# Two half quanta per slot, a later output tail in linear attention, query and key projections spread among the gates, and keys fetched in pieces, in a two-layer hybrid attention kernel

## The chip, the cores and the metric

The kernel runs on one core of one Trainium2 chip. The metric is device time in microseconds from start to end of one execution; the time before is the median of three runs.

## The reference

Two layers over 1024 latent tokens and 256 context tokens of width 1024; the output is the latents after the second layer. Per layer (`ctx` is the same with its own modulation, and has an output in the first layer only):

```python
h = rms_norm(x, norm_w) * (1.0 + scale) + shift
(na_q, na_k, na_v, gla_q, gla_k, gla_v, gla_g, ret_q, ret_k, ret_v, z, g) = split_cols(h @ w_in)
...
q = rms_norm(split_heads(q, NA_HEADS), q_norm); k = rms_norm(split_heads(k, NA_HEADS), k_norm)
na_l = neighbourhood_attention(ql, kl, vl, kc, vc, rpb)   # 8x16 windows on a 16x64 grid, plus all context keys
gla_l = bidir_scan(...)   # gated linear attention, a decay per key channel, forward and backward
ret_l = bidir_scan(...)   # retention, a fixed decay per head
y = sum(sigmoid(gs[i]) * ((outs[i] * silu(zs[i])) @ w_branch[i]) for i in range(3))
x = x + gate * (y @ w_out)
```

Columns of `w_in`: 3 × 512 for neighbourhood attention (8 heads of 64), 256 + 256 + 512 + 32 for linear attention, 1024 for retention, 1536 for z and 3072 for the gates g.

## The kernel before, in words

Every projection runs as a stream of matmuls in fp32 with weights split into a high and a low part (`whi`, `wlo`), three products per tile: activations' high part by both, their low part by `whi` (`fm_unit`, `tm_unit`, the matmul at L374 in `mms`). Weights come in groups of 256 columns; `conv` (L333) splits them on ACT (L340) and POOL (L343). A group of queries and keys, of gates or of z is two halves of 128 columns; in layer 0 each half runs over 512 + 512 + 256 tokens, in layer 1 the gates, z and the queries run over 512 + 512 only. One such block is a tile with its own bank of PSUM: three banks (`pg`) hold projection results, five (`pa`) hold those of the background.

The order of all instructions is written by hand, by a driver (`Drv`, L49 to L103). One generator yields the projections (`stream`), lanes yield the three branches, which spawn units ("workers"): retention chunks, linear attention chunks, neighbourhood attention units. A slot (`Drv.slot`, L81) steps each worker once, issues projection matmuls up to the quantum, runs late work and evacuations of finished tiles, steps the lanes, steps each worker again, runs the tail work, and last the weight loader. `mms` yields when `QUANT * drv.mult` columns are issued (L366): 6144 columns are twelve 512-wide matmuls. `drv.mult` is set by the branch that runs: 1.25 in retention, 1.1, 1.2 and 1.0 in linear attention (`GL_M`), 0.65 in neighbourhood attention (`NA_M1`). Linear attention falls from 1.2 to 1.0 once `d["done"]["nqk"]` is set (L857).

`projections` (L1089) takes, in this order: retention's, linear attention's and the values' columns, the four groups of queries and keys (`nqk`), twelve groups of gates, six of z. The fifth and sixth z group wait until the neighbourhood lane is at its end (`want_E`). A tile of queries or keys goes through `qk_evac` (L1151): COPY and Square on ACT (L1154, L1155), the mean over a head by a matmul with `blk` (L1160, `na_ms`), Ln, Exp and Square on ACT (L1162 to L1164), products on DVE (L1167 to L1182), the low part on POOL (L1186), and the stores of `nq`, `nkh`, `nkl` to DRAM. A gate tile is one Tanh (L1211, `st_g`).

Linear attention's `phase2` (L757) takes chunks of 128 tokens, one spawned every 8 slots. For seven levels it makes a decay (`dd`, exponential at L796), scaled queries and keys on DVE (`ek`, `eq`, L805 to L807) and a product on PE (`gla_lv`, L824), which ACT or DVE merges into `att`. Then come `gla_o` (L848) and `post` (L467): a copy into a staging buffer `posb`, mean squares on ACT and POOL, a scaling on DVE (L482), a transposition (`post_t`, L486), a gain and a store.

Neighbourhood attention (L863) goes over four pairs of heads; a pair has eight window units and, in layer 0, two context units. A unit (`pair`, L974) loads `q`, `qz` and the bias `bt`, then on PE: scores in four banks (`na_sw`, `na_sc`, L901, L902); softmax on DVE and ACT (L917 to L922 and L933 to L935); transposes (`na_ptw`, `na_ptc`, L944, L947); copies out on DVE and ACT (L966, L969, `PT`); and the product with the values (`na_o`, L1012). Each pair's `k0`, `k1` and `kl` (128 × 1280 floats each, 640 KB) are fetched during the pair before, one whole tile per unit from the fourth unit on, in the queue of SP.

## Time and profile before

| | |
|---|---|
| median of three runs | 3006.08 us (3004.04 to 3006.4) |
| the profiled execution | 3011.38 us |
| its span, first to last instruction | 3009.5 us |
| mean granted clock of TensorE | 0.976 |
| PE busy | 2850.7 us, 95% of the span |
| DVE, ACT, POOL busy | 1517.4, 1061.7, 1082.0 us |

Durations come from the profiled execution, which is 5.3 us above the median. PE's busy time counts matmuls; they overlap in the pipe, so a row's length is more than what it adds to the time: the distance between two rows' starts tells that. A wait is named by the instruction that waits and the one that released it.

### The profile page before, as it was taken

Reading aid. Unit: us, or ns where it says so; the run is one execution under the profiler, and the core shown is the slowest. Engines: PE = TensorE matmul, PEld = TensorE weight load, DVE = VectorE, ACT = ScalarE, POOL = GpSimd, SP = SyncE. Lnnn points to the kernel's source line nnn. Section 1 sums busy time; section 2 is a strip of 40 time slices with the busy share of each in tenths; the row PEclk is TensorE's granted clock in tenths of the full one; section 3 lists DMA queues with packets and bytes.
Section 4 is the critical chain, followed back from the end, with each engine's and each line's share of the span. In section 5 each row is a group of like instructions: output and inputs, shape, how many; then the busy total and the mean of one; then the engine's idle time right before and its main releaser. Section 6 shows DMA issues by size and latency. Waiting matters only on the chain. (4 is left out here: it accounts for less than half of the span.)

```text
span 3009.5 us, 52036 instructions
## 1 busy us (share of the span) xinstructions
PE 2850.7 (95%) x19776; PEld 2441.5 (81%) x19776; DVE 1517.4 (50%) x3261; ACT 1061.7 (35%) x2443; POOL 1082.0 (36%) x1010
## 2 busy tenths in 40 slices
PE   7999999899988899999999999999899978899999
PEld 5999987678877778778899999986677767777889
DVE  4147478866534555224333337378966255632431
ACT  5123465543333444212113223365544334432220
POOL 4222125565410102433655332115665210135463
PEclk8999999999999999999999999999899989999999
DMA  6244443433244454666445354443433445555633
GB/s 236 85 151 127 134 126 102 121 97 123 86 150 146 147 158 126 195 188 206 140 127 148 97 151 125 122 135 109 123 99 116 146 145 154 164 163 159 209 120 107
DMA packets 381161, 418.69 MB, mean 139 GB/s; under 512 B 33308, under 2 KB 298284, under 8 KB 380912
## 3 DMA queue, kind: packets, MB, share of 16 engines
q1 hardware_dynamic: 343552, 361.59, 39.9%
q10 hardware_dynamic: 37360, 53.79, 5.1%
q8 instruction: 156, 2.56, 0.4%
q14 instruction: 93, 0.76, 0.1%
HBM read 302.72 MB, written 112.54 MB: 138 GB/s over the span
## 5 line engine op out<-in xcount | busy, mean ns | idle before, releaser
L374 PE MATMUL fm<-h,whi 128*128 128x512 f32 (+1 forms) x3936 | 917.4, 379 | 0.0
L343 POOL TENSOR_TENSOR wlo<-wraw,whi 128x512 fp32r<-128x512 f32 (+1 forms) x336 | 461.5, 1394 | 1144.5 <-ACT whi L340 1086.5
L374 PEld LDWEIGHTS fm<-h,whi 128*128 128x128 f32 x3936 | 679.2, 191 | 142.8 <-issue 18.6
L374 PE MATMUL fm<-h,wlo 128*128 128x512 f32 (+1 forms) x1968 | 473.9, 378 | 0.0
L374 PEld LDWEIGHTS fm<-h,wlo 128*128 128x128 f32 x1968 | 342.5, 191 | 74.4 <-issue 12.2
L374 PE MATMUL tm<-whi,h 128*128 128x256 f32 (+1 forms) x2528 | 345.5, 285 | 2.4 <-ACT h L293 1.7
L374 PEld LDWEIGHTS tm<-whi,h 128*128 128x128 f32 x2528 | 321.4, 190 | 4.1 <-ACT h L293 2.1
L340 ACT CAST whi<-wraw 128x1024 fp32r<-128x1024 f32 (+1 forms) x168 | 175.4, 1047 | 289.4 <-PE tm L374 128.9
L374 PE MATMUL tm<-wlo,h 128*128 128x256 f32 (+1 forms) x1264 | 181.3, 285 | 0.0
L374 PEld LDWEIGHTS tm<-wlo,h 128*128 128x128 f32 x1264 | 164.2, 190 | 0.0
L1211 ACT ACTIVATE st_g<-fm 128x512 f32<-128x512 f32 (+1 forms) x120 | 66.5, 554 | 231.9 <-PE fm L374 177.0
L374 PE MATMUL tm<-whi,yy 128*128 128x256 f32 x1152 | 147.4, 280 | 0.0
L1227 DVE SCALAR_TENSOR_TENSOR st_z<-st_z,fm 128x512 f32<-128x512 f32 (+1 forms) x60 | 38.0, 634 | 214.5 <-ACT st_z L1226 211.7
L805 DVE TENSOR_TENSOR ek<-dd,kd 128x512 f32<-128x512 f32 x108 | 106.7, 988 | 68.8 <-ACT dd L796 68.5
L374 PEld LDWEIGHTS tm<-whi,yy 128*128 128x128 f32 x1152 | 140.8, 188 | 0.1
L781 POOL TENSOR_TENSOR dd<-Ac,ash 128x256 f32<-128x256 f32 x126 | 108.3, 860 | 88.3 <-DVE ash L768 56.8
L414 DVE COPY st_tm<-tm 128x256 f32<-128x256 f32 (+1 forms) x59 | 25.3, 429 | 174.0 <-PE tm L374 173.7
L824 PEld LDWEIGHTS gla_lv<-eq,ek 128*64 128x64 f32 x2016 | 70.8, 140 | 51.8 <-issue 29.9
L782 POOL TENSOR_TENSOR dd<-ash,Ac 128x256 f32<-128x256 f32 x126 | 110.9, 880 | 0.0
L1348 DVE TENSOR_TENSOR st_o<-tm,gb 128x256 f32<-128x256 f32 x72 | 30.5, 424 | 155.0 <-PE tm L374 120.7
L806 DVE SCALAR_TENSOR_TENSOR eq<-dd,g_col,qd 128x256 f32<-128x256 f32 x126 | 104.9, 832 | 6.5 <-ACT dd L796 6.5
L1294 DVE SCALAR_TENSOR_TENSOR gt<-gt,mg 128x512 f32<-128x512 f32 (+1 forms) x80 | 50.7, 634 | 110.9 <-PE mg L374 89.1
(1570 smaller groups left out, 4705.2 us busy)
## 6 DMA issues: line engine op xcount, KB each, us to landing
wraw<-in_w_in SPq DMA_DIRECT2D x104, 512.0 KB
wt<-in_w_mod SPq DMA_DIRECT2D x48, 512.0 KB
gd<-st_g ACTq DMA_DIRECT2D x96, 256.0 KB
gt<-gd SPq DMA_DIRECT2D x96, 256.0 KB
bt<-in_na_bm SPq DMA_DIRECT2D x32, 384.0 KB
ot<-o SPq DMA_DIRECT2D x48, 256.0 KB
wraw<-in_w_branch SPq DMA_DIRECT2D x24, 512.0 KB
k<-nkh SPq DMA_DIRECT2D x16, 640.0 KB
```

Source lines behind the costliest of these rows:

```text
L340: sc.copy(hi[:, :, :w], raw[:, :, :w])
L343: gp.tensor_tensor(lo[:, ks, :w], raw[:, ks, :w], fv(hi[:, ks, :w]), op=ALU.subtract)
L374: pe.matmul(ps, a(k), b(k), start=i == 0, stop=i == tot - 1)
L781: gp.tensor_tensor(dv[:, :, Lh:], av[:, :, Lh:], rv, op=ALU.subtract)
L782: gp.tensor_tensor(dv[:, :, :Lh], rv, av[:, :, :Lh], op=ALU.subtract)
L805: ve.tensor_tensor(ek_, E_, kd_, op=ALU.mult)
L806: ve.scalar_tensor_tensor(eq[:, :, Lh:], ev[:, :, Lh:], rsc, qv[:, :, Lh:], op0=ALU.mult, op1=ALU.mult)
L824: pe.matmul(pl_[bk, h, :], ek_[:, h, bk], eq_[:, h, bk if lv else bq], start=True, stop=True)
L1211: sc.activation(st[:, :nn], ps, AF.Tanh, scale=0.5)
L1227: ve.scalar_tensor_tensor(st[:, :nn], st[:, :nn], 1.0, ps, op0=ALU.add, op1=ALU.mult)
L1294: ve.scalar_tensor_tensor(gt[:, :nn], gt[:, :nn], 1.0, ps[:, :nn], op0=ALU.add, op1=ALU.mult)
L1348: ve.tensor_tensor(st[:, :256], ps, gbc[0 if t < LT else 1][:, 256 * gi:256 * gi + 256], op=ALU.mult)
```

## The change

A slot steps the workers, issues a half quantum (3072 columns times `drv.mult`), and does both again; late work, evacuations, lanes, tail and loader follow, and the second stepping of the workers behind the lanes is gone. `post` takes its buffer and two lags: retention keeps (2, 1), linear attention has (5, 2) and works in `att`. The exponential `qi` is written into `Ac`. `load_k` fetches five pieces of 256 tokens of each of its three tiles (128 KB each), three pieces per unit from the third unit on. In `projections` a group of queries and keys goes ahead of each of the first four pairs of gate groups, and `done["nqk"]` is set after the seventh gate group. In `qk_evac` the buffer `rs` is taken later and the mean-square product one step later. The list of groups, which sets the order of weight loading, follows.

```diff
--- before.py
+++ after.py
@@ -80,10 +80,11 @@
 
     def slot(self, gemm=True):
         self.n += 1
-        self._adv(self.workers)
         alive = False
-        if gemm:
-            alive = next(self.gemm, "end") != "end"
+        for _ in range(2):
+            self._adv(self.workers)
+            if gemm:
+                alive = next(self.gemm, "end") != "end"
         for f in self.late:
             f()
         self.late, self.later = self.later, []
@@ -91,7 +92,6 @@
             f()
         self.evq, self.evq_next = self.evq_next, []
         self._adv(self.lanes)
-        self._adv(self.workers)
         for f in self.tail:
             f()
         self.tail = []
@@ -363,7 +363,7 @@
                 load_raw()
             conv()
 
-    QUANT = 6144
+    QUANT = 3072
     acc = [0]
 
     def mms(ps, n, pairs, kd):
@@ -437,8 +437,12 @@
         G["gla"] = [add_group(wcols(1792, 256), KD), add_group(wcols(2048, 272), KD), add_group(wcols(2320, 272), KD),
                     add_group(wcols(1536, 256), KD)]
         G["nv"] = [add_group(wcols(1024, 256), KD), add_group(wcols(1280, 256), KD)]
-        G["nqk"] = [add_group(wcols(p * P, P) + wcols(512 + p * P, P), KD) for p in range(4)]
-        G["g"] = [add_group(wcols(5152 + 256 * i, 256), KD) for i in range(12)]
+        G["nqk"], G["g"] = [], []
+        for i in range(12):
+            if i % 2 == 0 and i < 8:
+                p = i // 2
+                G["nqk"].append(add_group(wcols(p * P, P) + wcols(512 + p * P, P), KD))
+            G["g"].append(add_group(wcols(5152 + 256 * i, 256), KD))
         G["z"] = {zi: add_group(wcols(3616 + 256 * zi, 256), KD) for zi in (2, 3, 4, 5, 0, 1)}
         G["wb"] = {br: [add_group([(A["w_branch"][layer, br][:, 256 * i:256 * i + 256], 256)], 4) for i in range(4)]
                    for br in BR_ORDER}
@@ -464,9 +468,8 @@
     xnew = [dr.tile([P, D], F32, tag=f"xn{t}", name=f"xn{t}") for t in range(NT)]
 
 
-    def post(pool, ops, gain, o_d, c):
+    def post(pool, ops, gain, o_d, c, osb, lag):
         ss = pool.tile([P, 12], F32, tag="pss", name="pss", bufs=2)
-        osb = stg("posb")
         on = osb.rearrange("p (h d) -> p h d", h=4)
 
         def squares():
@@ -477,15 +480,16 @@
             gp.tensor_scalar(ss[:, 4:8], ss[:, 0:4], 1.0 / P, EPS, op0=ALU.mult, op1=ALU.add)
             gp.tensor_tensor(ss[:, 8:12], ss[:, 4:8], mhalf, op=ALU.pow)
         drv.tail.append(squares)
-        yield
-        yield
+        for _ in range(lag[0]):
+            yield
         ve.tensor_tensor(on, on, ss[:, 8:12].unsqueeze(2).to_broadcast([P, 4, P]), op=ALU.mult)
-        yield
+        for _ in range(lag[1]):
+            yield
         pt = psa("post_t", (P, 4, P))
         for h in range(4):
             pe.transpose(pt[:, h, :], on[:, h, :], ident)
         yield
-        of = stg("pof")
+        of = osb if lag[0] > 2 else stg("pof")
         ve.tensor_tensor(of.rearrange("p (h t) -> p h t", h=4), pt, gain.unsqueeze(2).to_broadcast([P, 4, P]), op=ALU.mult)
         drv.defer(lambda: dma(o_d.rearrange("(h d) t -> d h t", d=P)[:, :, c * P:(c + 1) * P], of.rearrange("p (h t) -> p h t", h=4)))
 
@@ -619,7 +623,7 @@
                     pe.matmul(po[:, hs], att[:, h // 2, h % 2, :], v[:, hs], start=True, stop=False)
                     pe.matmul(po[:, hs], q2T[:, h // 2, h % 2, :], S[:, c, hs], start=False, stop=True)
                 yield
-                yield from post(pr, po, gain, d["o"][2], c)
+                yield from post(pr, po, gain, d["o"][2], c, stg("posb"), (2, 1))
 
             drv.mult = RT_M
             ws = []
@@ -809,7 +813,7 @@
                         vt = pl.tile([P, 512], F32, tag="v", name="vt", bufs=2)
                         dma(vt, d["gla"][c * P:(c + 1) * P, 0:512])
                     if i == 6:
-                        qi = stg("qi").rearrange("p (h t) -> p h t", h=4)
+                        qi = Ac
                         sc.activation(qi, Ac, AF.Exp, scale=s_pm)
                         ve.tensor_tensor(qi, qi, qd, op=ALU.mult)
                     yield
@@ -848,7 +852,7 @@
                     pe.matmul(po[:, hs], att[:, h, :], vt[:, hs], start=True, stop=False)
                     pe.matmul(po[:, hs], qi[:, h, :], S[:, c, hs], start=False, stop=True)
                 yield
-                yield from post(pl, po, gain, d["o"][1], c)
+                yield from post(pl, po, gain, d["o"][1], c, att.rearrange("p h t -> p (h t)"), (5, 2))
 
             ws = []
             for c in range(d["nt"]):
@@ -872,16 +876,17 @@
                 gp.memset(fv(qz[:]), 0.0)
 
             def load_k(p):
-                ks = []
-                for hd in range(2):
-                    k = pn.tile([P, NTOK], F32R, tag=f"k{hd}", name=f"k{hd}", bufs=2)
-                    r = p * P + 64 * hd
-                    dma(fv(k[:]), d["nkh"][r:r + 64, :].unsqueeze(0).to_broadcast([2, 64, NTOK]))
-                    ks.append(k)
-                    yield
+                ks = [pn.tile([P, NTOK], F32R, tag=f"k{hd}", name=f"k{hd}", bufs=2) for hd in range(2)]
                 kl = pn.tile([P, NTOK], F32R, tag="kl", name="kl", bufs=2)
-                dma(fv(kl[:]), d["nkl"][p * P:(p + 1) * P, :])
                 tiles["k", p] = ks, kl
+                for t0 in range(0, NTOK, 256):
+                    ts = slice(t0, t0 + 256)
+                    for hd in range(2):
+                        r = p * P + 64 * hd
+                        dma(fv(ks[hd][:, ts]), d["nkh"][r:r + 64, ts].unsqueeze(0).to_broadcast([2, 64, 256]))
+                        yield
+                    dma(fv(kl[:, ts]), d["nkl"][p * P:(p + 1) * P, ts])
+                    yield
 
             def load_v(p):
                 vcx = pn.tile([P, 2, P], F32, tag="vcx", name="vcx", bufs=2)
@@ -1048,7 +1053,7 @@
                 for n, unit in enumerate(heads(p)):
                     ws.append(drv.spawn(unit))
                     yield
-                    if n > 2:
+                    for _ in range(3 if n > 1 else 0):
                         next(nxt, None)
                     yield
                 for _ in nxt:
@@ -1150,12 +1155,14 @@
 
         def qk_evac(p):
             def f(m, t0, nn, ps):
-                raw, sq, rs = stg("nraw"), stg("nsq"), stg("nrs")
+                raw, sq = stg("nraw"), stg("nsq")
                 sc.copy(raw[:, :nn], ps)
                 sc.activation(sq[:, :nn], raw[:, :nn], AF.Square)
 
                 def w():
                     yield
+                    yield
+                    rs = stg("nrs")
                     pm_ = psa("na_ms")
                     pe.matmul(pm_[:, :nn], blk, sq[:, :nn], start=True, stop=True)
                     yield
@@ -1199,12 +1206,6 @@
                 drv.spawn(w())
             return f
 
-        for p in range(4):
-            yield from fm(G["nqk"][p], [ntok, NTOK], qk_evac(p))
-        yield
-        yield
-        d["done"]["nqk"] = True
-
         def g_evac(gi):
             def f(m, t0, nn, ps):
                 st = stg("st_g")
@@ -1214,7 +1215,11 @@
             return f
 
         for gi in range(12):
+            if gi % 2 == 0 and gi < 8:
+                yield from fm(G["nqk"][gi // 2], [ntok, NTOK], qk_evac(gi // 2))
             yield from fm(G["g"][gi], [ntok] * 2, g_evac(gi))
+            if gi == 6:
+                d["done"]["nqk"] = True
 
         def z_evac(zi):
             def f(m, t0, nn, ps):
```

What moves, in the order of the program. First ACT, in layer 0, where tiles of queries and keys are evacuated beside linear attention: `nraw` and the first `nsq` are COPY and Square of a tile, `nrs` its Ln and Exp, `dd` linear attention's exponential. Before (lines of the kernel before):

```order
L796 ACTIVATE dd<-dd 128x512
L1162 ACTIVATE nrs<-na_ms,eps_t 128x512
L1163 ACTIVATE nrs<-nrs 128x512
L1164 ACTIVATE nsq<-nrs 128x512
L1154 COPY nraw<-fm 128x256
L1155 ACTIVATE nsq<-nraw 128x256
L796 ACTIVATE dd<-dd 128x512
L1162 ACTIVATE nrs<-na_ms,eps_t 128x512
L1163 ACTIVATE nrs<-nrs 128x512
L1164 ACTIVATE nsq<-nrs 128x512
L340 CAST whi_6378<-wraw_6108 128x4x256
```

With the change, in a group that follows gates (L1169 is the Ln, L1170 the Exp):

```order
L800 ACTIVATE dd<-dd 128x512
L117 DMA gd_99<-st_g 128x256
L832 COPY near<-gla_lv 128x256
L800 ACTIVATE dd<-dd 128x512
L1169 ACT_TABLE_LOAD
L1169 ACTIVATE nrs<-na_ms,eps_t 128x512
L1170 ACT_TABLE_LOAD
L1170 ACTIVATE nrs<-nrs 128x512
L1171 ACTIVATE nsq<-nrs 128x512
L1159 COPY nraw<-fm 128x512
L1160 ACTIVATE nsq<-nraw 128x512
L1159 COPY nraw<-fm 128x256
```

Between a tile's Ln and its Exp, and ahead of the Ln, stand loads of ACT's table that were not there; in the whole program the loads go from 5 to 71.

Second, PE in linear attention's chunks of layer 0: the level products (`gla_lv`) and the projection matmuls between them. Before, after the queries and keys:

```order
L824 MATMUL gla_lv<-eq,ek 64x64 x8
L374 MATMUL fm<-h_0_141,whi_6378 128x512 x4
L374 MATMUL fm<-h_4_142,whi_6534 128x512 x4
L374 MATMUL fm<-h_8_143,whi_6378 128x512 x4
L824 MATMUL gla_lv<-eq,ek 64x64 x8
L374 MATMUL fm<-h_12_144,whi_6534 128x512 x4
L374 MATMUL fm<-h_0_141,wlo_6379 128x512 x4
L374 MATMUL fm<-h_4_142,wlo_6535 128x512 x4
L824 MATMUL gla_lv<-eq,ek 64x64 x8
```

With the change, among the gates and the remaining queries and keys:

```order
L828 MATMUL gla_lv<-eq,ek 64x64 x8
L374 MATMUL fm<-h_0_141,whi_7297 128x512
L374 MATMUL fm<-h_4_142,whi_7510 128x512 x4
L374 MATMUL fm<-h_8_143,whi_7297 128x512 x4
L374 MATMUL fm<-h_12_144,whi_7510 128x512 x4
L374 MATMUL fm<-h_0_141,wlo_7298 128x512 x3
L828 MATMUL gla_lv<-eq,ek 64x64 x8
```

Between two level products stood 12 projection matmuls, and now stand 16 as long as `nqk` isn't done.

Third, PE in neighbourhood attention of layer 0. Before, between all units of the stage:

```order
L901 MATMUL na_sc<-k_9439,q 128x256
L902 MATMUL na_sc<-kl,qz_8960 128x256
L374 MATMUL fm<-h_0_141,wlo_9562 128x512 x4
L374 MATMUL fm<-h_4_142,wlo_9753 128x512 x4
L944 MATMUL na_ptw<-ident,P__10612 128x128 x3
L947 MATMUL na_ptc<-ident,P__10612 128x128 x2
L944 MATMUL na_ptw<-ident,P__10619 128x128 x3
L947 MATMUL na_ptc<-ident,P__10619 128x128 x2
L374 MATMUL fm<-h_0_145,whi_9561 128x512 x4
L374 MATMUL fm<-h_4_146,whi_9752 128x512 x4
L1012 MATMUL na_o<-PT,vw 64x128 x6
L1012 MATMUL na_o<-PT,vcx 64x128 x4
```

With the change, the last projection matmuls of the stage (the fourth z group's) and what follows them:

```order
L374 MATMUL fm<-h_8_150,whi_10452 128x256 x4
L374 MATMUL fm<-h_8_150,whi_10622 128x256 x4
L374 MATMUL fm<-h_0_149,wlo_10453 128x256 x4
L374 MATMUL fm<-h_0_149,wlo_10623 128x256 x4
L1017 MATMUL na_o<-PT,vw 64x128 x6
L1017 MATMUL na_o<-PT,vcx 64x128 x4
L906 MATMUL na_sw<-k_10838,q 128x384
L907 MATMUL na_sw<-kl,qz_9351 128x384
L906 MATMUL na_sw<-k_10839,q 128x384
L907 MATMUL na_sw<-kl,qz_9351 128x384
L906 MATMUL na_sc<-k_10838,q 128x256
L907 MATMUL na_sc<-kl,qz_9351 128x256
```

From there the units' products follow one another without a projection matmul, over 13 window units and 4 context units in layer 0, and over 19 window units in layer 1; before, projection matmuls stood between the units in both layers to the end of the stage.

## Rows read from the trace of the kernel before

**Rows 1.** The page's first part: span, and busy time of each engine.

```profile
span 3009.5 us, 52036 instructions
PE 2850.7 (95%) x19776; PEld 2441.5 (81%) x19776; DVE 1517.4 (50%) x3261; ACT 1061.7 (35%) x2443; POOL 1082.0 (36%) x1010
```

**Rows 2.** PE's waits over the whole span: the waiting instruction, what released it, us in total, number, longest.

```profile
PE na_o L1012 <- ACT PT L969: 47.6, 7, 14.5
...
PE post_t L486 <- DVE posb L482: 14.6, 5, 5.7
PE gla_lv L824 <- DVE eq L807: 13.9, 8, 4.1
...
PE na_ms L1160 <- ACT nsq L1155: 9.3, 5, 3.6
```

**Rows 3.** Stretches of the span: length, busy us of PE, PEld, DVE, ACT and POOL (instructions), granted clock, DMA share, GB/s. Linear attention with queries and keys in layer 0, neighbourhood attention in layer 0, and both in layer 1.

```profile
400.00:650.00 250.00, 226.59 (x1544) 179.41 (x1543) 207.25 (x349) 135.40 (x267) 126.94 (x126) 0.97 0.38 111
850.00:1160.00 310.00, 277.26 (x1965) 236.06 (x1964) 165.08 (x537) 128.45 (x421) 27.44 (x21) 0.94 0.49 150
1950.00:2200.00 250.00, 227.38 (x1540) 182.18 (x1539) 204.77 (x363) 136.35 (x257) 116.05 (x106) 0.97 0.41 116
2350.00:2660.00 310.00, 270.18 (x1791) 224.36 (x1790) 170.56 (x511) 119.81 (x386) 36.89 (x27) 0.92 0.51 155
```

**Rows 4.** The chain of waits in neighbourhood attention of layer 1: start, us, what.

```profile
2391.87 17.55 DMA k<-nkh
...
2478.82 24.30 DMA k<-nkh
```

**Rows 5.** ACT's groups between 400 and 650 us, the instructions of a tile of queries or keys: busy us, mean ns of one, idle before.

```profile
L1162 ACT ACTIVATE nrs<-na_ms,eps_t 128x512 f32<-128x512 f32 (+1 forms) x24 | 14.6, 610 | 22.1 <-DVE nraw L1172 5.3 <-PE na_ms L1160 4.2 <-DVE Sg L501 2.8
L1163 ACT ACTIVATE nrs<-nrs 128x512 f32<-128x512 f32 (+1 forms) x24 | 13.5, 561 | 0.8
L1155 ACT ACTIVATE nsq<-nraw 128x512 f32<-128x512 f32 (+1 forms) x24 | 13.5, 561 | 8.7 <-DMA nq<-nrs 1.9 <-DVE nraw L1182 1.9 <-DMA nkh<-nrs 1.9
L1164 ACT ACTIVATE nsq<-nrs 128x512 f32<-128x512 f32 (+1 forms) x24 | 13.5, 561 | 0.8
...
L1154 ACT COPY nraw<-fm 128x512 f32<-128x512 f32 (+1 forms) x24 | 12.2, 509 | 14.0 <-DMA nq<-nrs 6.3 <-PE fm L374 4.8 <-DMA nkh<-nrs 2.3
```

**Rows 6.** ACT's timeline at two loads of its table: start, us, instruction, in brackets the idle time before it.

```profile
324.65 0.38 ACT L1083 ACTIVATE st_fm<-fm 128x256 f32<-128x256 f32 x1 [0.37 <-PE fm L374]
...
325.07 1.28 ACT L743 ACT_TABLE_LOAD   x1
...
591.84 1.28 ACT L1211 ACT_TABLE_LOAD   x1 [1.33 <-DMA nkl<-nraw]
```

**Rows 7.** PE's timeline over one chunk of linear attention in layer 0.

```profile
764.75 0.60 PE L486 MATMUL post_t<-ident,posb 128*128 128x128 f32 x4
...
784.13 2.01 PE L374 MATMUL fm<-h,wlo 128*128 128x512 f32 x8
785.99 0.38 PE L848 MATMUL gla_o<-vt,att 128*128 128x128 f32 x2
...
794.97 0.60 PE L486 MATMUL post_t<-ident,posb 128*128 128x128 f32 x4
```

**Rows 8.** The stretch from 650 to 793 us (columns as in rows 3), linear attention beside gates, and in it ACT's gates and weight casts.

```profile
650.00:793.00 143.00, 143.00 (x1163) 116.99 (x1163) 93.51 (x147) 56.89 (x136) 79.83 (x91) 1.00 0.34 106
...
L1211 ACT ACTIVATE st_g<-fm 128x512 f32<-128x512 f32 (+1 forms) x22 | 11.6, 529 | 60.6 <-PE fm L374 60.5
L340 ACT CAST whi<-wraw 128x1024 fp32r<-128x1024 f32 x7 | 7.3, 1039 | 0.0
```

**Rows 9.** The timeline around one unit of neighbourhood attention in layer 0: start, us, engine, instruction.

```profile
1013.99 0.40 PE L901 MATMUL na_sw<-k,q 128*128 128x288 f32 x1
...
1015.10 2.02 PE L374 MATMUL fm<-h,wlo 128*128 128x512 f32 x8
...
1016.76 0.46 ACT L921 ACTIVATE P__10712<-na_sc,nst 128x256 f32<-128x256 f32 x1
1016.97 0.49 PE L944 MATMUL na_ptw<-ident,P__10612 128*128 128x128 f32 x3
...
1017.51 0.49 PE L944 MATMUL na_ptw<-ident,P__10619 128*128 128x128 f32 x3
...
1018.21 0.64 ACT L969 COPY PT<-na_ptc 128x256 f32<-128x256 f32 x2
...
1020.01 0.88 PE L1012 MATMUL na_o<-PT,vw 128*64 128x128 f32 x12
...
1021.25 0.39 PE L901 MATMUL na_sc<-k,q 128*128 128x256 f32 x1
```

**Rows 10.** PE's timeline at a unit's scores under the lower clock.

```profile
894.52 0.61 PE L901 MATMUL na_sw<-k,q 128*128 128x288 f32 x1
...
896.51 2.48 PE L374 MATMUL fm<-h,whi 128*128 128x256 f32 x16
```

**Rows 11.** PE's timeline at the start of the program, and two stretches there (columns as in rows 3).

```profile
15.45 0.61 PE L208 MATMUL mod_ps<-wt,csi 128*2 128x256 f32 x8 [0.67 <-DMA wt<-in_w_mod]
...
15.00:16.00 1.00, 0.55 (x8) 0.11 (x8) 0.00 (x0) 0.00 (x0) 0.00 (x0) 1.00 0.99 397
17.00:18.00 1.00, 0.70 (x8) 0.00 (x0) 0.84 (x2) 0.00 (x0) 0.00 (x0) 0.50 1.04 414
```

More of the change, by code (lines that the diff above doesn't have):

```diff
@@ L874, in load_k @@
             def load_k(p):
-                ks = []
-                for hd in range(2):
-                    k = pn.tile([P, NTOK], F32R, tag=f"k{hd}", name=f"k{hd}", bufs=2)
-                    r = p * P + 64 * hd
-                    dma(fv(k[:]), d["nkh"][r:r + 64, :].unsqueeze(0).to_broadcast([2, 64, NTOK]))
-                    ks.append(k)
+                ks = [pn.tile([P, NTOK], F32R, tag=f"k{hd}", name=f"k{hd}", bufs=2) for hd in range(2)]
+                kl = pn.tile([P, NTOK], F32R, tag="kl", name="kl", bufs=2)
+                tiles["k", p] = ks, kl
+                for t0 in range(0, NTOK, 256):
[5 more added lines that the diff above has]
+                    dma(fv(kl[:, ts]), d["nkl"][p * P:(p + 1) * P, ts])
                     yield
-                kl = pn.tile([P, NTOK], F32R, tag="kl", name="kl", bufs=2)
-                dma(fv(kl[:]), d["nkl"][p * P:(p + 1) * P, :])
-                tiles["k", p] = ks, kl
             def load_v(p):
```

## The prediction

> **What bounds the kernel now.** I read the page's busy times first, then the waits of PE, then PE's busy time by stage, then the chain of waits, and last single units in the timeline. TensorE (PE) is busy for 2850.7 of 3009.5 us [rows 1]: it is the bound, and all that a new order of the same work can win is the 159 us in which it stands still, and what its clock loses around those gaps. The reader is to see in the waits that the idle time has few causes [rows 2]: the na_o product of the neighbourhood attention waits 47.6 us in 7 waits, post_t (the output tail) 14.6, gla_lv (the level products of linear attention) 13.9, na_ms (the mean square of queries and keys) 9.3. By stage [rows 3], linear attention together with the query and key projections leaves PE idle for 250 − 226.59 = 23.4 us in layer 0 and 22.6 in layer 1, 46 together; neighbourhood attention for 32.7 and 39.8, 73 together. Granted clock below 1 costs more: busy time times the missing share is (226.59 + 227.38) × 0.03 = 13 us in the first stage; in the second 277.26 × 0.06 + 270.18 × 0.08 = 38, of which I count 25, since part of the low clock lies in gaps where PE had nothing to run (the 25 is a choice). So the change can touch **59 us** in the first stage and **98 us** in the second. In the second stage the chain names the cause [rows 4]: the steps of 17.55 and 24.30 us are landings of whole key tiles.
>
> **The change, part by part.** *Half quanta.* A slot now issues projection work in two halves with a step of the background units ahead of each. A unit steps twice per slot as before, but between a step's softmax or decay work and the product that reads it there is no longer a pair of steps with no projection between them. That addresses the gla_lv and na_ms waits: 13.9 + 9.3 at most. *Later tail.* gla's post waits 5 and 2 steps in place of 2 and 1, into the att tile, which lives longer: this takes the 14.6 us of post_t, and since a chunk starts every 8 slots and att has two buffers, I cost the longer life at nothing. Moving qi into Ac removes a buffer and no work. *Keys in pieces.* Fifteen transfers per pair in place of three of 640 KB, three per unit, from the third unit on: SP issues 12 more per pair; spread over units of 7.3 us (1013.99 to 1021.25 [rows 9]) I cost them at nothing. If that cover is gone, in the uncovered units below, the next pair's keys come late, which is the upper bound there.
>
> *Spread query and key projections.* The order on ACT shows what this adds: 71 table loads stand in the program, 5 before. Where a query or key tile follows gates, its Ln and its Exp each get a load, so two for each of 18 + 15 = 33 tiles. Four contiguous groups need none; before, one load ahead of the first gate was enough. A load takes 1.28 us [rows 6], and 66 of them 85 us of ACT. To see what reaches PE I compare ACT and PE per tile. ACT: the five instructions of a tile, 509 + 561 + 610 + 561 + 561 ns [rows 5], are 2.80 us; two loads 2.57; the casts of weights 2 × 1.04 per group of 6 tiles, 0.35; linear attention's own. A chunk of that takes 794.97 − 764.75 = 30.2 us [rows 7], 8 slots; in 143 us of that stage ACT is busy for 56.89, of which 11.6 are gates and 7.3 casts [rows 8]: 38.0, so 8.0 us per chunk, 1.0 per slot. PE: eight 512-wide matmuls take 785.99 − 784.13 = 1.86 us [rows 7], 0.2325 each; a tile has 20 on the mean (24 of a full one, 12 of the half-wide fifth), 4.65 us; and a chunk's 8 slots × 12 × 0.2325 = 22.3 leave 7.9 of background, 1.0 per slot, 1.25 per tile at the 16 matmuls that a slot now holds. So ACT needs 2.80 + 2.57 + 0.35 + 1.25 = 7.0 us per tile against 5.9 on PE: an excess of 1.1 × 33 = 36 us, less what ACT may fall behind before PE stands, which I put at about half a tile, 2.7 us (a choice: projection results have three banks), at each of 6 bursts, 16: **20 us** of stall. With low clock around these (as before, 13 per 46: 6 us) and with the first group of each layer unchanged, a quarter of the 59, 15: 41 us in place of 59, **−18**. Bounds: below, all stalls gone, −59. Above, each load with the idle time that stands ahead of the nearest row, 1.33 us before the load at 591.84 [rows 6]: 2.7 more per tile, 33 × 3.8 − 16 = 109, clock by the same share 31, and the 15 make 155, +96. I take 1.28, because at 325.07 the load stands directly behind the instruction before it, without a gap, and the 1.33 is put down to other work.
>
> The Trainium skill speaks against this part (ScalarE: Activation LUTs, What ACT_TABLE_LOAD costs and Rules for kernel authors): a switch of sets costs the load of about 1283 ns and a drain of about 1380 ns, 2.66 us, and calls should be batched by set. The trace agrees on the load, and has the gap in one place but not at the other; by that figure the loads would take 66 × 2.66 = 176 us of ACT in place of 85.
>
> *Work used up earlier.* Slots under linear attention now hold 16 matmuls to the end of the seventh gate group, where they fell to 12 once queries and keys were done. The same projections therefore end earlier against the background, and z groups past the fourth must wait for the neighbourhood attention's end. In the new order of PE this stage's tail has no projection matmul: from PE's rows, 13 window units and 4 context units of layer 0 and 19 window units of layer 1 stand one behind the other. Before, every one had 16 between. What such a unit takes uncovered, from the timeline of one [rows 9]: scores start at 1013.99; ACT's exponential of the second head that frees a score bank ends about 1017.3 (1016.76 + 0.46 and the read of its sum), 3.3 us; the transposes of a head behind it 0.55 (1016.97 to 1017.51); ACT's copy ends 0.8 after the transposes (1018.21 + 0.64 against 1017.51 + 0.54), and na_o is 1.24 (1020.01 to 1021.25). Together that is **6.0 us** with 0.1 for the hand-overs, of which PE works for 1.11 + 2 × 0.54 + 1.24 = 3.4 and is idle for 2.6. A context unit goes through the same chain without the window's part; I count 2.5 idle for it, and 4.5 per layer for the drain of the last units, both estimates from that chain. 32 × 2.6 + 4 × 2.5 + 9 = 102 us. The clock: where PE had work for 0.61 of each 1.28 us the granted clock was 1.00 at first and 0.50 from 17 us on [rows 11], in which scores take 896.51 − 894.52 = 1.99 us [rows 10] in place of 1.11. At the lower clock a unit's three pieces add about 2 us; over 36 units 72, and I take half, 36, between a clock kept and a clock lost throughout. Bounds: below, DVE alone, 165.08 us for 40 units [rows 3], 4.1 us and 0.7 idle, 22 and 10 for the context units; above, the full 174.
>
> *What is left.* With 10 us of the old key waits in the covered part: 102 + 36 + 10 − 98 = **+50**. Other stages: same work, nothing.
>
> **Sum.** −18 + 50 = +32 against the profiled execution's 3011.4, so 3043; that run is 5 us above the median of the three shown, 3006.1, so I forecast **3038 us**, slower.
>
> **Rivals.**
> - *Faster, on the clock.* The uncovered units keep the upper clock, and the spread tiles are absorbed by gates between bursts so that only the first groups' 15 us stay: 102 + 10 − 98 − 44 = −30, about 2976; with DVE's bound per unit it would be 70 less. It decides at 106 us for the uncovered tail with the first stage at −18, or 132 with it at −44; the chain alone gives 102. For: DVE and ACT are busy for only 165 and 128 of 310 us there [rows 3]. Against: PE's order puts a unit's transposes behind the next unit's scores, and both share five banks.
> - *Table switches with gap, much slower.* Each costs the load and 1.33: +96 in place of −18, about 3152. For: ACT works in order, with gla's exponentials behind the loads. Against: the load at 325.07. The Trainium skill's rule (ScalarE: Activation LUTs, What ACT_TABLE_LOAD costs) would act in this way.
> - *No change.* The clock stays up and the tiles are as forecast: −18 + 14 = −4, about 3002.
> - *The pieces do nothing.* Keys arrive no earlier, since the units of the uncovered tail run on faster than the loads: up to 17 us more per pair, and some 60 more than the forecast: 3098.
>
> **How the numbers follow.** Forecast 0.45 (its own range 3015 to 3070), faster 0.25, much slower 0.12, no change 0.10, pieces 0.08. About 0.2% (6 us) is what a measurement of this kernel can tell from no change. The range 2970 to 3120 takes in the forecast and most of the first, third and last rival. From the cases: faster 0.28 (a little of the third rival), same 0.08, slower 0.64.
>
> **What would show it.** In the changed profile: some 71 table loads of 1.28 us; PE idle in the tail of each neighbourhood attention at 2 to 3 us per unit, with no projection row; waits of na_ms and of projection tiles on ACT; gla_lv and post_t waits nearly gone, na_o waits on keys short. It is wrong if the last 40 us of window units show PE over 80% busy, or if tables stall ACT and PE by over 50 us.

## The result, and the profile after

The changed kernel takes 3030.53 us (median of four runs, 3028.30 to 3036.17) against 3005.82 us (median of four): a ratio of 1.0083 (95% interval 1.0067 to 1.0099), 25 us slower. Forecast were 3038 us. The profiled execution took 3036.17 us; like that of before it lies between 5 and 6 us above its median, so the two traces can be set against each other. The page after, span and busy time of each engine:

```profile
span 3034.4 us, 52017 instructions
PE 2875.9 (95%) x19776; PEld 2451.8 (81%) x19776; DVE 1509.2 (50%) x3261; ACT 1140.0 (38%) x2509; POOL 1074.3 (35%) x1010
```

Against [rows 1] the span is 24.9 us longer, and PE's busy time 25.2 us (2875.9 against 2850.7), with the same 19776 matmuls: idle time is the same in all, 158.5 us against 158.8, and has moved. ACT is busy for 78 us more. Of PE's waits (us in total, number, longest):

```profile
PE na_ptw L949 <- ACT oN L1020: 22.5, 5, 6.8
...
PE na_o L1017 <- ACT PT L974: 13.6, 7, 3.8
PE na_ms L1167 <- ACT nsq L1160: 12.3, 5, 5.3
...
PE na_sw L906 <- DMA q<-nq: 11.0, 5, 3.8
PE gla_lv L828 <- DVE eq L811: 10.5, 9, 2.0
...
PE post_t L490 <- ACT dd L800: 6.4, 1, 6.4
PE post_t L490 <- DVE att L485: 6.0, 5, 2.4
```

Against [rows 2], na_o's waits are down from 47.6 to 13.6, and post_t's from 14.6 to 12.4 in two rows. gla_lv's row is down from 13.9 to 10.5, but with its smaller rows gla_lv stands 17.4 us, more than before. na_ms's are up from 9.3 to 12.3, and the longest are now the transposes' (na_ptw) behind oN, with 11.0 us of scores behind a fetch of q (10.7 before).

To compare equal work, the stretches must hold the same projection matmuls. From the first matmul of the queries and keys to the first of the z group that waits for neighbourhood attention (of the order 2, 3, 4, 5, 0, 1 that is the third, number 4; the kernel's description and the prediction put it later) the work is the same in both. The first score divides each such stretch. Columns: length, PE, PEld, DVE, ACT, POOL busy, granted clock, DMA share, GB/s. Before, layer 0 and layer 1:

```profile
399.34:861.95 462.61, 434.17 (x3107) 350.10 (x3104) 316.98 (x518) 208.12 (x433) 223.19 (x232) 0.98 0.36 108
861.95:1219.78 357.83, 329.60 (x2308) 280.37 (x2309) 184.87 (x587) 145.11 (x463) 45.80 (x37) 0.95 0.49 149
1984.64:2381.95 397.31, 369.06 (x2422) 288.08 (x2420) 274.02 (x440) 179.79 (x357) 202.57 (x196) 0.97 0.38 112
2381.95:2686.66 304.71, 270.52 (x1824) 224.72 (x1825) 175.16 (x519) 122.35 (x392) 45.12 (x34) 0.93 0.52 160
```

After:

```profile
399.92:972.95 573.03, 542.28 (x3650) 441.59 (x3649) 319.01 (x519) 275.32 (x504) 242.49 (x248) 0.98 0.36 106
972.95:1242.81 269.86, 237.11 (x1770) 196.91 (x1768) 181.77 (x588) 124.26 (x432) 32.46 (x27) 0.95 0.54 160
2005.30:2483.60 478.30, 458.87 (x2830) 361.62 (x2828) 275.60 (x441) 236.14 (x413) 219.26 (x214) 0.99 0.39 116
2483.60:2711.41 227.81, 189.35 (x1417) 153.98 (x1416) 166.08 (x520) 103.78 (x366) 27.41 (x21) 0.92 0.57 167
```

Layer 0 goes from 820.4 to 842.9 us, layer 1 from 702.0 to 706.1, everything else together from 1487.0 to 1485.4. Adding PE's idle time and the time that the lower clock cost (in each sample of the clock, busy time by the missing share) gives, in us, over both layers:

| | before | after |
|---|---|---|
| queries and keys to the first score: idle and clock | 72.0 | 63.4 |
| first score to z: idle and clock | 88.7 | 95.4 |
| PE busy, put at the full clock, both | 1361.8 | 1390.3 |
| sum | 1522.5 | 1549.1 |

So linear attention with the projections gained 9 us, and neighbourhood attention lost 7 and the 28 us by which PE's busy time grew. That growth is no work, since the matmuls are the same. In the uncovered tail (the units without projection matmuls between them) a product starts before all of its inputs are there, and the wait lies inside a row that counts as busy; na_o shows it (busy us, mean ns, idle before). Before, then after:

```profile
L1012 PE MATMUL na_o<-PT,vw 96*64 96x128 f32 (+1 forms) x768 | 56.6, 281 | 0.0
...
L1012 PE MATMUL na_o<-PT,vcx 128*64 128x128 f32 x576 | 49.9, 288 | 47.6 <-ACT PT L969 47.6
```

```profile
L1017 PE MATMUL na_o<-PT,vw 96*64 96x128 f32 (+1 forms) x768 | 75.7, 295 | 10.9 <-DVE PT L971 6.9 <-ACT PT L974 2.3 <-issue 0.3
...
L1017 PE MATMUL na_o<-PT,vcx 128*64 128x128 f32 x576 | 59.8, 292 | 11.4 <-ACT PT L974 11.4
```

The two groups of each kernel overlap in time. With each moment counted once, na_o is busy for 96.3 us before and 116.1 after, 20 us more, and the transposes ahead of it (na_ptw, na_ptc) for 11 us more; part of both is the lower clock. How the tail runs, from PE's timeline in layer 0 (start, us):

```profile
1155.46 0.40 PE L906 MATMUL na_sw<-k,q 128*128 128x288 f32 x1
...
1156.59 0.49 PE L949 MATMUL na_ptw<-ident,P__11930 128*96 128x128 f32 x3
...
1157.66 0.53 PE L949 MATMUL na_ptw<-ident,P__11937 128*96 128x128 f32 x3 [0.36 <-DVE nst L922]
...
1158.71 1.23 PE L1017 MATMUL na_o<-PT,vw 96*64 96x128 f32 x11 [0.29 <-DVE PT L971]
...
1160.49 0.44 PE L906 MATMUL na_sw<-k,q 128*128 128x384 f32 x1
...
1168.00 0.45 PE L906 MATMUL na_sw<-k,q 128*128 128x384 f32 x1 [1.80 <-DMA q<-nq]
...
1177.86 0.61 PE L906 MATMUL na_sw<-k,q 128*128 128x288 f32 x1 [3.83 <-DMA q<-nq]
```

From score to score an uncovered unit takes 1160.49 − 1155.46 = 5.03 us, and where queries come late, 9.86 (1168.00 to 1177.86). Eleven na_o matmuls take 1.23 us at 1158.71, where twelve take 0.88 in a covered unit [rows 9]. Cut where the late fetches end, the two tails are (columns as above; layer 0, then layer 1):

```profile
1139.40:1202.00 62.60, 45.38 (x336) 36.83 (x336) 43.36 (x148) 28.34 (x104) 5.89 (x5) 0.86 0.56 162
1202.00:1242.81 40.81, 34.59 (x295) 26.60 (x292) 32.94 (x116) 22.27 (x83) 0.00 (x0) 0.99 0.34 99
2584.80:2662.00 77.20, 52.56 (x381) 42.46 (x380) 52.03 (x165) 30.22 (x111) 5.69 (x5) 0.80 0.60 178
2662.00:2711.41 49.41, 42.81 (x373) 33.48 (x373) 42.11 (x146) 27.32 (x102) 0.00 (x0) 1.00 0.38 112
```

In the first part of each tail, units wait for fetches, PE idles for 17.2 and 24.6 us, and the granted clock averages 0.86 and 0.80. In the second part PE is busy for 34.6 of 40.8 and 42.8 of 49.4 us and the clock is 0.99 and 1.00, nearly all at the upper of its two levels. DVE, with 32.9 and 42.1 us, is almost as busy as PE.

Of the tables, the lines and one tile, on ACT:

```profile
L1169 ACT ACT_TABLE_LOAD x33 | 42.3, 1283 | 10.6 <-DMA nq<-nrs 7.6 <-DVE nraw L1185 1.6 <-DVE nraw L1179 0.9
L1170 ACT ACT_TABLE_LOAD x33 | 42.3, 1283 | 0.6
```

```profile
522.42 1.28 ACT L1169 ACT_TABLE_LOAD   x1
525.43 0.69 ACT L1169 ACTIVATE nrs<-na_ms,eps_t 128x512 f32<-128x512 f32 x1 [1.72 <-PE na_ms L1167]
526.13 1.28 ACT L1170 ACT_TABLE_LOAD   x1
527.43 0.63 ACT L1170 ACTIVATE nrs<-nrs 128x512 f32<-128x512 f32 x1
```

66 loads are there (L1169, L1170), and the 33 of L1170 stand straight behind the Ln with 0.6 us of idle time in all.

### The profile page after: what moved, and what is told of

Its sections match the earlier page's. It is cut to its first block, busy times and chain, and to the rows that moved or that the text cites. A ratio compares the mean times of both kernels' runs of the same rounds, so it can differ in the third digit from the quotient of the medians.

```text
span 3034.4 us, 52017 instructions
## 1 busy us (share of the span) xinstructions
PE 2875.9 (95%) x19776; PEld 2451.8 (81%) x19776; DVE 1509.2 (50%) x3261; ACT 1140.0 (38%) x2509; POOL 1074.3 (35%) x1010
## 4 chain that ended last, share of the span: by engine, by line
PE 53%; DVE 6%; DMA 5%; issue 4%; POOL 2%; ACT 2%; SPq 1%; ACTq 0%; POOLq 0%; DVEq 0%
PE fm L374 23%; PE tm L374 10%; PE mg L374 9%; DMA k<-nkh 2%; PE na_o L1017 2%; SPq L114 1%; POOL wlo L343 1%; PE gla_lv L828 1%; DVE nst L924 1%; POOL st_o L1354 1%; DMA vw<-nv 1%; PE na_sw L906 1%; DMA kl<-nkl 1%; PE mod_ps L208 1%; PE na_ptw L949 1%
## 5 line engine op out<-in xcount | busy, mean ns | idle before, releaser
L374 PEld LDWEIGHTS fm<-h,whi 128*128 128x128 f32 x3936 | 679.7, 190 | 147.2 <-issue 17.2
L374 PE MATMUL tm<-whi,h 128*128 128x256 f32 (+1 forms) x2528 | 337.1, 284 | 3.5 <-ACT h L293 2.0
L374 PE MATMUL tm<-wlo,h 128*128 128x256 f32 (+1 forms) x1264 | 188.0, 286 | 0.0
L1242 POOL TENSOR_TENSOR br<-st_z,br 128x512 fp32r<-128x512 f32 (+1 forms) x20 | 23.7, 1189 | 250.4 <-ACT br L1241 250.4
L800 ACT ACTIVATE dd<-dd 128x512 f32<-128x512 f32 x126 | 78.5, 628 | 79.0 <-POOL dd L786 78.9
```

The source lines that it names most:

```text
L374: pe.matmul(ps, a(k), b(k), start=i == 0, stop=i == tot - 1)
L800: sc.activation(E_, E_, AF.Exp)
```

## Experiments

Twelve kernels, each timed beside the kernel before, in several sessions; since its median was 3006 to 3010 us in them, differences below are taken between ratios, at 30 us for each 0.01. With no other word an edit is made to the changed kernel.

**Cover under neighbourhood attention (e1).**

```diff
-NA_M1 = 0.65
+NA_M1 = 0.33
```

> The changed kernel with NA_M1 0.33 in place of 0.65: a unit of neighbourhood attention is covered by 8 projection matmuls in place of 16, so that the projections last over all 40 units of layer 0 and all but 5 of layer 1. Theory (the uncovered tail of 17 + 19 units is what costs the time: each stands 1.5 to 2 us at PE): 8 matmuls are 1.86 us and fit into that standing, so some 32 x 1.6 = 50 us are won against the changed kernel, 2980 us, below the kernel before. Rival (the table loads or the key pieces cost the time, the uncovered units don't): 3020 to 3035.

3010.09 us, ratio 1.0006 (0.9996 to 1.0016): 23 us won of 50. One unit of it, and one of PE's waits:

```profile
2637.71 0.40 PE L906 MATMUL na_sw<-k,q 128*128 128x288 f32 x1
...
2638.82 1.09 PE L374 MATMUL fm<-h,whi 128*128 128x512 f32 x4
...
2640.75 1.17 PE L374 MATMUL fm<-h,whi 128*128 128x512 f32 x4
...
2643.09 0.40 PE L906 MATMUL na_sw<-k,q 128*128 128x288 f32 x1
```

```profile
PE na_sw L906 <- DMA q<-nq: 27.2, 11, 4.5
```

With 8 matmuls a unit takes 5.38 us, only 0.35 more than uncovered, and 8 matmuls are 1.86 us [rows 7]: an uncovered unit does stand for some 1.5 us, as expected. But the units now wait for queries, 27.2 us against 11.0. These 16 us are more than half of the 27 that are missing; where the rest went is not shown.

**One table set (e2).**

```diff
-sc.activation(st[:, :nn], ps, AF.Tanh, scale=0.5)
+sc.activation(st[:, :nn], ps, AF.Exp if gi < 7 else AF.Tanh, scale=0.5)
```

> The changed kernel with an exponential in place of the tanh in the first seven gate groups, so that those gates share a table set with the queries' and keys' Ln and Exp and the program's table loads go from 71 back to 5; order and instructions are the same otherwise. It leaves out the right value of these gates (7 of 12 groups). Theory (a load costs 1.28 us of ACT and PE waits for 20 to 26 us of the 85): 3005 to 3011. Rival by the Trainium skill (ScalarE: Activation LUTs, What ACT_TABLE_LOAD costs), 2.66 us per switch: 60 us or more are won, below 2970. Rival, loads hidden beside PE: 3028 to 3033.

2997.78 us, 0.9969 (0.9958 to 0.9981): 34 us below the changed kernel. The stretch to the first score falls from 573.0 to 550.0 us in layer 0 and from 478.3 to 465.9 in layer 1; the tail doesn't move. The loads cost the kernel 34 of their 85 us, more than the 20 to 26 expected and far from the 60 or more of the rival. By the account of the table above, 30.2 us of idle time and clock are left up to the first score, of 63.4.

**Short start (e5), and whole keys (e4).** The pieces have one more effect: the first pair's 16 fetches, one per slot, put the first unit 13 slots later, with 12 matmuls in each.

```diff
-            for _ in both(0):
-                yield
+            for i, _ in enumerate(both(0)):
+                if i % 5 == 4:
+                    yield
```

> The changed kernel with the first pair's 16 fetches issued five per slot, so that neighbourhood attention starts 13 slots earlier; keys still come in pieces. Its order has 8 + 8 uncovered units in place of 17 + 19. Theory (uncovered units cost some 1.6 us each): 20 x 1.6 = 32 us are won, about 2998. Rival (what costs the time lies elsewhere): 3025 to 3035.

3014.65 us, 1.0016 (1.0006 to 1.0025): 20 us won of 32. The uncovered units fall to 8 + 8, but the first scores of both layers now wait for fetches (5.8 and 3.0 us).

For whole keys `load_k` and its call are those of before.

> The changed kernel with keys fetched as whole tiles again, one per unit from the fourth on, and hence the short start: coverage as in the run with the short start (8 + 8 uncovered units). Theory (pieces take away most of the 98 us that the key landings cost before, for the units that are covered): 20 to 60 us above the run with the short start, 3020 to 3060. Rival (pieces do nothing by themselves, since the same bytes go through the same queue): within 5 us of it, about 2998.

3057.69 us, 1.0166 (1.0151 to 1.0181): 45 us above the short start with the same cover. PE's waits with whole keys, then in pieces:

```profile
PE na_o L1016 <- ACT PT L973: 44.1, 8, 16.3
```

```profile
PE na_o L1017 <- ACT PT L974: 25.0, 10, 6.1
```

The pieces also go out from the third unit on in place of the fourth, so this compares size and order of the fetches together.

**Contiguous queries and keys (e3).** The groups' order, the list of weights and the buffer and product step of `qk_evac` are those of before; the flag stays behind the seventh gate group.

```diff
-            if gi % 2 == 0 and gi < 8:
-                yield from fm(G["nqk"][gi // 2], [ntok, NTOK], qk_evac(gi // 2))
+        for p in range(4):
+            yield from fm(G["nqk"][p], [ntok, NTOK], qk_evac(p))
```

> The changed kernel with the four groups of queries and keys contiguous ahead of the gates again (and their buffer and product step as before the change); the flag nqk is still set after the seventh gate group, so that the uncovered units stay 17 + 19. Table loads are 5. The run with one table set stood 33 us below the changed kernel. Theory A (half quanta and the later tail take away the stalls of linear attention, the spread adds only its loads): as that run, 2992 to 3004. Theory B (the spread itself takes away the stalls, which come back in one burst): 3015 to 3045.

3016.75 us, 1.0034 (1.0022 to 1.0045), at the lower edge of theory B: 15 us below the changed kernel, 19.5 above the run with one table set. The spread, together with the step and buffer change of `qk_evac`, wins 19.5 us and its loads cost 34.

**Half quanta alone (e7)**, in the kernel before: the slot and `QUANT` of the change.

> The kernel before with half quanta alone (the slot and the size of the quantum). Neighbourhood attention is covered throughout. Theory A (they take most of the gla_lv, na_ms and post_t waits, 38 us, with their share of low clock): 2965 to 2985. Theory B (waits follow the number of slots, which is unchanged): 2998 to 3010.

3085.62 us, 1.0261 (1.0246 to 1.0276): both theories fell, it is 78 us slower. PE's waits:

```profile
PE post_t L486 <- DVE posb L482: 58.2, 17, 7.4
...
PE na_ms L1160 <- ACT nsq L1155: 21.6, 8, 6.0
...
PE fm L374 <- ACT st_g L1211: 12.4, 2, 6.6
PE gla_lv L824 <- DVE eq L807: 7.2, 4, 4.9
```

gla_lv's waits are halved, as the theory had it, but post_t's go from 14.6 to 58.2, na_ms's from 9.3 to 21.6, and gates are evacuated late. The stretch to the first score loses 89 + 64 us to idle time and clock, 72 before; 52 of these 153 us are clock, 15 before.

**Short tail (e9)**, the contiguous variant with:

```diff
-att.rearrange("p h t -> p (h t)"), (5, 2))
+stg("posb"), (2, 1))
```

> The contiguous variant with linear attention's tail at lags 2 and 1 and in a staging buffer as before the change; the uncovered units are 16 and 17 in place of 17 and 19. Theory (the later tail takes the post_t waits, 14.6 us before): 8 to 15 us above the contiguous run. Rival (the tail's waits vanish with half quanta anyway): 3 us below to 3 above it.

3063.41 us, 1.0186 (1.0171 to 1.0201): 46 us above the contiguous run. Its wait, 11.8 us in that run:

```profile
PE post_t L490 <- DVE posb L485: 43.4, 16, 6.9
```

The later tail is what makes half quanta bearable.

**Covered throughout (e8)**, the contiguous variant with the flag behind the queries and keys and `NA_M1 = 0.5`.

> The contiguous variant with the flag nqk set right behind the queries and keys as before the change and NA_M1 0.5: every unit of neighbourhood attention has 12 projection matmuls, no table loads are added, half quanta, key pieces and the later tail stay. Theory (uncovered units cost 1.45 us each, loads 33 in all; what is left are fetches at the pairs' boundaries): 2998 - 52 and up to 20 of waits for fetches, 2950 to 2970. Rival (units are bound by fetches as soon as they run faster): 2985 to 3000.

3010.49 us, 1.0010 (1.0001 to 1.0020): 7 us below the contiguous run, on the rival's side and above even its 2985 to 3000. Neighbourhood attention and its tail took 30 us less, but linear attention, at 12 matmuls a slot again, stood 24 us more (74 against 50 us of idle time and clock). Cover moved is not cover won.

**Pieces alone (e10)**, in the kernel before: `load_k` and its call as changed, with the short start.

> The kernel before with keys in pieces alone (three per unit from the third unit on; the first pair's fetches five per slot, so that neighbourhood attention starts in the same slot as before). Slots, tail and projection order stay; all units have 16 matmuls. Theory (pieces are worth 43 us, as between the runs with whole keys and with the short start, and need neither half quanta nor the other parts): 2960 to 2975. Rival (with whole quanta the fetch waits come from something else, q and the bias): 2995 to 3010.

2979.51 us, 0.9895 (0.9880 to 0.9910): 32 us below the kernel before, where 43 were expected. From the first score to z, both layers:

```profile
868.99:1208.16 339.17, 324.93 (x2310) 276.13 (x2308) 185.27 (x587) 144.35 (x462) 45.84 (x37) 0.97 0.51 154
2373.38:2659.62 286.24, 266.75 (x1825) 221.62 (x1824) 173.71 (x519) 122.06 (x391) 42.09 (x32) 0.96 0.55 167
```

339.2 + 286.2 us against 357.8 + 304.7, 37 us less. The stretches ahead of the first scores became 10 us longer: just before the scores PE waits 8.6 and 8.5 us for the evacuation of gates (st_g), where the first scores had waited 5.0 and 5.6 us for fetches of the bias and of queries. Whether the size of the pieces or their earlier start wins the time was not tried apart.

**Cover moved (e11)**: the same with `GL_M = (1.1, 1.2, 1.2)`, `NA_M1 = 0.5`.

> The same, and cover moved from neighbourhood attention to linear attention: GL_M 1.2 throughout, NA_M1 0.5, so 12 matmuls per unit (enough for the 1.5 us that an uncovered unit stands) and 14 or 15 per slot of linear attention. Theory (both stages stand less when cover lies where it is needed): 5 to 20 us below the run with pieces alone. Rival (shorter units only wait for fetches): 3 below to 10 above it.

3007.47 us, 0.9992 (0.9982 to 1.0002): 29 us above pieces alone. Linear attention stood 11 us less, neighbourhood attention 32 more (81 against 49 us of idle time and clock). Its chain of waits shows what a unit of 6.3 us runs into:

```profile
2412.47 7.84 DMA wraw<-in_w_in
2420.32 8.25 DMA k<-nkh
...
2438.45 8.07 DMA k<-nkh
```

Weights (512 KB) and a key piece (128 KB) land one behind the other, 7.8 and 8.3 us.

**Half quanta, covered (e12)**, the contiguous variant with the short start and `NA_M1 = 0.5`.

> The contiguous variant of the changed kernel (half quanta, later tail, pieces, 16 matmuls to the seventh gate group) with the short start and NA_M1 0.5: every unit but the last has 12 matmuls. Theory (uncovered units cost 1.45 us each, 36 of them 52, the short start gives back 14 at the first keys, and shorter units wait some 10 more for fetches): 3017 - 52 + 24 = 2989, between 2980 and 2998. Rival (cover under neighbourhood attention is worth nothing): 3010 or more.

3003.96 us, 0.9979 (0.9967 to 0.9992): 16 us below the contiguous run, 28 expected, and just below the kernel before.

**Pieces and the later tail (e13)**: e10 with the changed `post`, its call and `qi`.

> The kernel before with keys in pieces and the short start, as the run with pieces alone, and with linear attention's later tail (lags 5 and 2, in the att tile, qi in Ac); whole quanta, contiguous queries and keys. Theory (the later tail takes the post_t waits of 14.7 us and what low clock goes with them, under whole quanta too): 8 to 18 us below the run with pieces alone, 2962 to 2972. Rival (the later tail only repairs what half quanta break, and the longer life of att holds up the next chunks): 2 below to 10 above it.

2972.80 us, 0.9891 (0.9875 to 0.9908), the lowest median of all; but by ratios it is 1 us below pieces alone, in the rival's range, and the intervals overlap: a gain of the later tail under whole quanta isn't shown. post_t still waits 14.7 us.

## Why the prediction was right, and where its steps were not

Direction, size and both stages' signs came out: −18 and +50 were forecast, −9 and +35 measured, −2 elsewhere. Inside, several steps were wrong and cancelled; that the forecast came within 8 us is in part luck. Both stages before were also read from parts of them: 59 and 98 us were to be touched, 72 and 89 stand in the whole stretches.

- **Half quanta** were to win up to 23 us of gla_lv and na_ms waits. Alone they lose 78 (e7), and in the changed kernel both groups wait longer than before. The step failed on what it left out: the tail's and the mean square's products come due too soon for DVE and ACT.
- **The later tail** was to win post_t's 14.6 us. It repairs 46 us of what half quanta break (e9); post_t's waits end at 12.4.
- **Table loads**: 1.28 us each and no gap, as chosen; 26 us with clock were forecast, 34 measured (e2). The drain, and with it the Trainium skill's price (ScalarE: Activation LUTs, What ACT_TABLE_LOAD costs), shows in none of the 33 loads behind a Ln, nor in the time. Its rule to group calls by set (Rules for kernel authors) holds by the load alone. The rival with a gap at each load fell with it. Of the stage's other stalls, 15 us were to stay; 30 do (e2). The spread takes away stalls without its loads (19.5 us, e3 against e2), but the sum let three quarters of the 59 go without saying which part of the change takes them.
- **The uncovered tail**: 17 + 19 units, as read from the order, but the cause was half seen: with the short start 8 + 8 are left (e5), so the pieces' 13 slots make more than half of it, not the 16 matmuls alone. The period of undisturbed units is 5.0 to 5.3 us where 6.0 was forecast, since the first head's transposes start right behind the scores (1156.59) and don't wait for a bank, as the chain's sum made them: 36 units of 1.5 us are some 54 us, not 102. By the prediction's own sign this step was wrong: at the end of layer 1 PE is 87% busy by its rows (42.8 of 49.4 us), over the 80% named, and idles by its rows for less than 1 us a unit in place of 2 to 3, though a part of the busy time is waits inside rows. Of the 36 us of clock, 18 came, nearly all in the parts of the tails that wait for fetches. In all the tails hold some 101 us (55 idle, 18 clock, and the 28 inside rows, if all of these lie there), where 138 were forecast. What is above the 54, some 47, is put down to late fetches and the clock around them, since the parts of the tails that hold them have 42 of the 55 us of idle time; the sum had them only in a rival and an upper bound.
- **Keys in pieces** were to leave 10 us of the old waits in the covered part; 23 are left there (16.5 idle, 6 clock). Covered throughout and with 16 matmuls, pieces leave 49 of 89 (e10); the faster the units, the more of each fetch shows (e8, e11, e12). So the tails were put 37 us too high, the covered part 13 too low, and 9 too much was taken off for the kernel before: together the 15 us by which +50 lies above +35.
- **Rivals.** The pieces did a lot: 45 us at the same cover (e4), 32 alone; but the units of the tail did outrun their fetches, as the last rival had it. The clock was kept where no fetch was late, as the faster rival had it, and the fetches took its gain.

Added up one by one (pieces −32, half quanta +78, later tail −46, loads +34, spread −19.5, late start +20) the parts give +34 where 25 were measured; each was measured beside other parts, so the sum need not close. It leaves out the 16 matmuls per slot up to the seventh gate group, which win time in linear attention and cost it in the tail (24 against 30 us in e8, with cover of 12 for every unit). How the step and buffer changes in `qk_evac` share in it was not separated, nor why the clock falls so much in e7.

## What to carry to other kernels

When units of a background hide behind a stream of matmuls, count what every other edit does to the place where the stream runs out: a fetch loop with a yield per piece delayed the first unit by 13 slots, and cover spent in one stage is missing in the next. Try each part of a change alone: the one good part here (keys in pieces, 32 us) was outweighed by parts that needed each other. And when the units get faster, look at the fetches before counting the gain.

## What was not expected of the hardware

- A table load costs ACT 1283 ns and nothing around it here: 33 loads behind a Ln with 0.6 us of idle time in all. Some were loaded while ACT waited anyway (522.42, ahead of a wait of 1.72 us).
- A 640 KB key fetch was the step that released the next work after 17.55 and 24.30 us [rows 4]; the pieces of 128 KB that the chain of e11 shows took 8.1 and 8.3 us, a fifth of the bytes in a third to a half of the time.
- PE's busy time is not its work: with the same 19776 matmuls it grew by 25 us, and na_o's rows by 20.
- A store that ACT issues can hold up its copies, and PE behind them. In the four longest waits of na_ptw behind oN, ACT had stood 7.9 to 11.1 us until, by the profile, a fetch of keys or values landed; then it issued the store of `o` and made the copy. The longest na_o wait of before, 14.5 us, has the same form with the store of a gate. Why the store's issue stands while fetches are under way, no run here shows. Before, then after (layer 1):

```profile
2431.05 0.33 ACTq L117 DMA_DIRECT2D gd<-st_g  x1
2431.42 0.65 ACT L969 COPY PT<-na_ptc 128x256 f32<-128x256 f32 x2 [15.89 <-DMA vcx<-nv]
```

```profile
2600.46 0.33 ACTq L117 DMA_DIRECT2D o<-oN  x1
2600.83 0.27 ACT L1020 COPY oN<-na_o 128x128 f32<-128x128 f32 x1 [9.17 <-DMA vw<-nv]
```
